# Residual of the last norm kept in the output and added there by accumulating transfers

## The chip, the cores and the metric

The kernel runs on one core of a Trainium2 chip. The metric is the device time of one execution in microseconds. Engines are called PE (TensorE), DVE (VectorE), ACT (ScalarE), POOL (GpSimd) and SP (SyncE); SP begins nearly all transfers.

## What is computed

One decoder block on x of 1024 rows by 1024 columns, float32. A token-mixing part (two kinds of attention) gives x2; then comes the channel part, at whose end the change lies:

```python
x = x + gt_a * rms_norm(y, g_attn_post[l])           # x2 below

h = rms_norm(x, g_mlp_pre[l]) * (1 + sc_m) + sh_m
y = jnp.square(jax.nn.relu(h @ w_up[l])) @ w_down[l]
x = x + gt_m * rms_norm(y, g_mlp_post[l])            # the output
```

rms_norm divides each row by the root of its mean square and multiplies by a gain. The kernel holds gt_m times the gain as one tile, `gate_m`.

## The kernel before

Rows are worked on in eight blocks of 128 (tb 0 to 7), one row to a partition. Every product is made of three float32r passes over a high and a low part of its operands (lines 2103 to 2105). The two products of the channel part are cut into quadrants and multiplied by a scheme with seven products in place of eight (P1 to P7), over eight steps h; ACT writes the high parts (L1864), DVE the low parts (L1871). Sums of the second product collect in eight tiles `yacc0` to `yacc7` of 128 x 1024, to which DVE adds each finished 128 x 512 piece from PSUM (L2161).

The order of instructions is set while the program is built. A planner (`Sched`) holds a queue for each engine, with an estimated duration, dependencies, buffers taken and given, and a priority for each step; it always emits the step that could begin first by its estimates. So a changed step can move others. On the chip each engine runs its list in order and waits on semaphores.

What the change touches:

- `out_rest(tb, ...)` ends the token-mixing part of a block. It stores x2 of the block in a scratch tensor `x2_dram[tb]` (L1724, 512 KB).
- `finish(tb, n, e)` runs when columns 512n to 512n + 511 of block tb are complete, so twice for each block. ACT squares the piece and sums each row (`f_sq`, L2178) into a column of a small tile `st3`.
- At a block's first call DVE multiplies the piece by `gate_m` in place (L2186), adds a small constant to the sum (L2182), and SP begins the load of x2 from scratch into `x2_sb` (L2191).
- At the second call DVE multiplies that piece by `gate_m` into a tile `yg` (L2198), adds the two sums (L2201), POOL raises the result to -1/2 (L2203), and DVE does for each half `x2_sb = half * power + x2_sb` in one operation (L2205). SP stores each half of 256 KB to the output (L2211).

In the last step (h = 7) the last products are P3, P7 and P4. P7 completes the first pieces of blocks 4 to 7, and P4, the very last, their second pieces, block by block.

Of the kernel before, what the change touches and what calls it, by code (L numbers as in the profile page):

```python
# [10 lines left out]
F32 = mybir.dt.float32  # L11
# [4 lines left out]
ALU = mybir.AluOpType  # L16
# [3 lines left out]
P = 128  # L20
# [3 lines left out]
TB = S // P  # L24
# [172 lines left out]
class Sched:  # L197
# [18 lines left out]
    def op(self, eng, dur, emit, deps=(), **kw):  # L216

        o = self.step(dur, emit, deps, **kw)
        o.alts = None
        if isinstance(eng, str):  # L220
            self.queue[eng].append(o)
        else:
            o.alts = dict(zip(eng, zip(dur, emit)))
            for e in eng:
                self.queue[e].append(o)
        return o.ev

    def pe_op(self, stream, dur, emit, deps=(), **kw):
        o = self.step(dur, emit, deps, **kw)
        o.alts = None  # L230
        self.pe.setdefault(stream, []).append(o)
        return o.ev
# [104 lines left out]
def t_sb(n):  # L337
    return 0.098 + 0.00083 * n


def t_as(n):
    return 0.2 + 0.00083 * n


def t_dv(n):
    return 0.066 + 0.00104 * n
# [14 lines left out]
AP_COST = 0.093  # L361
AP_DV = 0.066
# [3 lines left out]
def hybrid_block(ctx: ExitStack, tc: tile.TileContext, x, positions, w_ada, b_ada, g_attn_post, w_in, w_out,  # L366
                 g_mlp_post, w_up, w_down, ada_t, consts, out):
    nc = tc.nc
    ctx.enter_context(tc.manual_schedule())
    V, A, G, T = nc.vector, nc.scalar, nc.gpsimd, nc.tensor  # L370
    x, out = x[0], out[0]
    w_ada, w_out, w_up, w_down = w_ada[0], w_out[0], w_up[0], w_down[0]
    sc = Sched()
    op, pe_op = sc.op, sc.pe_op
# [13 lines left out]
    def ring_l(name, dtype=F32R):  # L388

        return ph2.left.tile([P, 1024], dtype, name=name, tag="left")  # L390

    def ring_r(name):

        return ph2.right.tile([P, 1024], F32, name=name, tag="right")
# [7 lines left out]
    r_stg, r_w, r_wl, r_hl = Res(NSTG), Res(WR), Res(WR + 1), Res(0)  # L402
    r_u, r_raw, r_h2 = Res(0), Res(0), Res(0)
# [12 lines left out]
    nhalf = const.tile([P, KC], F32, name="nhalf")  # L416
# [15 lines left out]
    x2_dram = [dram.tile([P, D], F32, name=f"x2_dram{i}") for i in range(TB)]  # L432
# [27 lines left out]
    def stage(name):  # L460
        if st.stgp is None:
            return ring_r(name)
        return st.stgp.tile([P, 1024], F32, name=name, tag="stg")

    def load(emit, nbytes, deps=(), takes=(), prio=5, gives=(), after=None, n=1):
        return op("SP", nbytes / 345e3, emit, deps, takes=takes, prio=prio, gives=gives, after=after, kind=n)
# [121 lines left out]
    e = op("ACT", 0.1, lambda: A.activation(cond[:], c_raw, AF.Exp, scale=-1.0), [e_c], prio=0)  # L588
# [13 lines left out]
    e = op("DVE", 1.3, f_diag, [e_cond], takes=[(r_wa, 1)], prio=0)  # L602
# [7 lines left out]
    e = pe_op("mod", 1.7, f_cps, [e, e_init], takes=[(r_t, 2)], gives=[(r_wa, 1)])  # L610
# [17 lines left out]
    cs = p0.tile([64, 3, P], F32, name="cs")  # L628
# [8 lines left out]
    e = e_pos  # L637
    for f in steps:
        e = op("DVE", 0.13, f, [e, e_c], prio=8)
# [908 lines left out]
    def out_block(tb):  # L1548
# [83 lines left out]
        def products(m):  # L1632
# [5 lines left out]
            for n, i, k in order:  # L1638
# [29 lines left out]
                else:  # L1668
# [3 lines left out]
                    ey.append(op("DVE", t_dv(512) + AP_DV, f_yb, [e, ea[n], er[1]], gives=[(r_b, 1)], prio=0))  # L1672
        me.load, me.products = load_o, products
        me.rest = lambda: out_rest(tb, b, late, ey, f_lx)
        return me

    def out_rest(tb, b, late, ey, f_lx):
        ex = load(f_lx, 524288, takes=[(r_vb if tb < 2 else r_stg, 1)], prio=-3)

        def f_sq(col, first):  # L1680
            def f():
                if first:
                    b["st"] = small.tile([P, 4], F32, name="st2", tag="st2")
                A.activation(ph2.junk[:], b["y"][:], AF.Square, accum_out=b["st"][:, col:col + 1])
            return f

        def norm(col, dep):
            bx = []

            def f1():  # L1690
                t = small.tile([P, 8], F32, name="rs_t", tag="rs_t")
                bx.append(t)
                V.tensor_scalar(t[:, :1], b["st"][:, col:col + 1], 1.0 / D, EPS, ALU.mult, ALU.add)
            def f2():
                G.tensor_tensor(b["st"][:, col + 1:col + 2], bx[0][:, :1], nhalf[:, :1], ALU.pow)

            def whole():
                f1()
                f2()
                V.tensor_copy(bx[0][:, 1:2], b["st"][:, col + 1:col + 2])  # L1700

            def joined():
                f1()
                f2()
                f_gate()
                f_res()
            if tb == TB - 1:
                if col:
                    return op("DVE", 1.0, whole, [dep], prio=-1)
                return op("DVE", 0.8 + 2 * t_dv(D), joined, [dep, ph2.e_gate, ex], gives=[(r_u, 1), (r_stg, 1)], prio=-1)  # L1710
            e = op("DVE", 0.08, f1, [dep], prio=0)
            return op("POOL", 1.4, f2, [e], prio=0)
        e = op("ACT", t_sb(D) + AP_COST, f_sq(0, True), ey, prio=1)
# [5 lines left out]
        e = norm(0, e)  # L1719
        if tb < TB - 1:  # L1720
            e = op("DVE", t_dv(D), f_gate, [e, ph2.e_gate], prio=1)
            e = op("DVE", t_dv(D), f_res, [e, ex], gives=[(r_stg, 1)] if tb > 1 else [], prio=1)
            ph2.e_res.append(e)
        e_x2[tb] = load(lambda: nc.sync.dma_start(x2_dram[tb][:], b["y"][:]), 524288, [e], prio=-2)  # L1724
        e = op("ACT", t_sb(D) + AP_COST, f_sq(2, False), [e], prio=1)
        e = norm(2, e)

# [6 lines left out]
        for kg in range(2):  # L1734
            def f_t(kg=kg):
                b["px", kg] = pt.tile([P, 4, P], F32, name="px2", tag="t")
                for k in range(4):
# [3 lines left out]
                            gives=[(r_u if tb == TB - 1 else ph2.r_xn, 1)] if kg else []))  # L1741
        half, tq = divmod(tb, TB // 2)
        for kg in range(2):
# [3 lines left out]
            def f_ev(eng, kg=kg, q=q):  # L1747
                def f():
# [12 lines left out]
            e = op(("DVE", "ACT"), (1.0, 1.2), (f_ev(V), f_ev(A)), [et[kg]] + [e_mod[g] for g in (2, 3, 4, 5)] +  # L1761
                   (e_h2[q][-1:] if tq else []),
                   takes=[(r_h2, 2)] if tq == 0 else [], gives=[(r_t, 1)], prio=1)
# [3 lines left out]
    e_x2 = {}  # L1767
# [27 lines left out]
    ml = Tok()  # L1795
# [372 lines left out]
    def finish(tb, n, e):  # L2168


        first = tb not in ml.st
        s = ml.st.setdefault(tb, Tok())
        cs = slice(512 * n, 512 * n + 512)

        def f_sq():
            if first:
                s.t = small.tile([P, 4], F32, name="st3", tag="st3", bufs=TB)
            A.activation(ph2.junk[:, :512], ml.y[tb][:, cs], AF.Square, accum_out=s.t[:, n:n + 1])  # L2178
        late = 0 if tb >= TB // 2 and not first else 100
        esq = op("ACT", t_as(512) + 0.19, f_sq, [e] + ([] if first else [s.e0]), prio=1 + late)  # L2180
        if first:
            s.e0 = op("DVE", 0.16, lambda: V.tensor_scalar(s.t[:, n:n + 1], s.t[:, n:n + 1], D * EPS, None, ALU.add),  # L2182
                      [esq], prio=3 + late)
            s.n0 = n
            s.yg = {n: lambda: ml.y[tb][:, cs]}
            s.eg = [op("DVE", t_dv(512), lambda: V.tensor_tensor(ml.y[tb][:, cs], ml.y[tb][:, cs], ml.gate[:, cs],  # L2186
                                                                 ALU.mult), [esq, ml.e_gate], prio=4 + late)]

            def f_lx():
                s.x = stage("x2_sb") if tb < TB // 2 else ring_r("x2_sb")  # L2190
                nc.sync.dma_start(s.x[:], x2_dram[tb][:])  # L2191
            r = r_stg if tb < TB // 2 else r_raw
            s.ex = load(f_lx, 524288, [e_x2[tb]], takes=[(r, 1)], prio=900 + tb)
            return

        def f_g():
            s.g = ring_l("yg", F32)
            V.tensor_tensor(s.g[:, 0:512], ml.y[tb][:, cs], ml.gate[:, cs], ALU.mult)  # L2198
        s.yg[n] = lambda: s.g[:, 0:512]
        s.eg.append(op("DVE", t_dv(512), f_g, [e, ml.e_gate], takes=[(r_u, 1)], prio=1 + late))  # L2200
        e = op("DVE", 0.16, lambda: V.tensor_tensor(s.t[:, 2:3], s.t[:, 0:1], s.t[:, 1:2], ALU.add), [esq, s.e0],  # L2201
               prio=late)
        e = op("POOL", 0.55 if tb == TB - 1 else 1.5, lambda: G.tensor_tensor(s.t[:, 3:4], s.t[:, 2:3], nhalf[:, :1], ALU.pow), [e], prio=0)  # L2203
        for i, hf in enumerate((s.n0, 1 - s.n0)):
            e1 = op("DVE", t_dv(512) + AP_DV, lambda hf=hf: V.scalar_tensor_tensor(  # L2205
                s.x[:, 512 * hf:512 * hf + 512], s.yg[hf](), s.t[:, 3:4], s.x[:, 512 * hf:512 * hf + 512],
                ALU.mult, ALU.add), [e, s.ex] + s.eg, prio=late)

            def sent(i=i):
                ml.done += i  # L2210
            load(lambda hf=hf: nc.sync.dma_start(out[tb * P:(tb + 1) * P, 512 * hf:512 * hf + 512],  # L2211
                                                 s.x[:, 512 * hf:512 * hf + 512]), 262144, [e1],
                 gives=[(r_u, 1)] if i else [], prio=-1, after=sent)

    RAW = ("11", "21", "12", "22")

# [68 lines left out]
```

## Time and profile before

| What | Value |
| --- | --- |
| Median of 3 runs | 1118.76 us (1116.28 to 1120.53) |
| The profiled execution | 1117.71 us |
| Its span, first to last instruction | 1115.9 us |
| Mean granted PE clock | 0.997 |
| Last matmul begins | 1106.41 us into the span |
| Last store begins | 1112.8 us into the span |

A row of the timeline gives the start in us from the span's beginning, the duration, the engine, the line and the operation as output <- inputs. A bracket at its end gives how long the engine sat idle before it, and what ended that. A row on a line or an operation gives min, median and max duration in ns, and the first and last start. A row on DMA issues gives the count, the size of one, and the median us from issue to landing. Durations of neighbours on one engine overlap a little, since one operation begins while the last one's writes end.

### The profile page before, as it was taken

What the parts mean: (1) busy time and instruction counts of PE and PEld (TensorE: products, weight loads), DVE (VectorE), ACT (ScalarE), POOL (GpSimd) and SP (SyncE); (2) the same over time, 40 slices, a digit from 0 to 9 for tenths busy, and PEclk for the clock granted to TensorE, in tenths of its full rate; (3) what the DMA queues carried; (4) which work ended last, traced back from release to release, by engine and by line L of the source; (5) the groups of instructions that cost most, each with busy time, mean ns of one, the idle gap of its engine ahead of it and who ended that gap; (6) DMA issues with size and microseconds to landing.
All of it is one profiled execution on the core that took longest, in us unless ns stands there. A gap on an engine that the chain in (4) does not pass through costs nothing.

```text
span 1115.9 us, 15870 instructions
## 1 busy us (share of the span) xinstructions
PE 1095.1 (98%) x5512; PEld 919.8 (82%) x5512; DVE 846.2 (76%) x1487; ACT 645.2 (58%) x1149; POOL 168.6 (15%) x215
## 2 busy tenths in 40 slices
PE   7999999999999999999999999999999999999996
PEld 6889888888998878888888888888888888888885
DVE  8975876899878976789698653898644996527998
ACT  7826576688867757587674334743145632347542
POOL 1003245456542322110000000000000000000002
PEclk9999999999999999999999999999999999999999
DMA  9767748677636517635851378511578013584104
GB/s 358 258 213 233 185 140 257 194 220 231 179 110 205 147 58 240 212 143 226 323 214 38 113 254 320 189 57 43 197 266 314 21 57 113 189 321 150 38 19 151
DMA packets 98585, 200.75 MB, mean 180 GB/s; under 512 B 8456, under 2 KB 31560, under 8 KB 98504
## 3 DMA queue, kind: packets, MB, share of 16 engines
q1 hardware_dynamic: 98504, 199.73, 53.0%
q8 instruction: 44, 0.72, 0.3%
q14 instruction: 37, 0.30, 0.1%
HBM read 157.56 MB, written 42.14 MB: 179 GB/s over the span
## 4 chain that ended last, share of the span: by engine, by line
PE 79%; DVE 10%; ACT 4%; DMA 3%; issue 3%; SPq 0%; POOL 0%; DVEq 0%; POOLq 0%; ACTq 0%
PE mlp_ps L2104 17%; PE mlp_ps L2105 17%; PE mlp_ps L2103 17%; PE pj L931 2%; PE pj L934 2%; PE pj L932 2%; PE s_ps L1215 2%; PE y_ps L1648 2%; PE y_ps L1649 2%; PE y_ps L1650 2%; PE s_ps L1269 1%; PE o_ps L1349 1%; PE o_ps L1360 1%; PE acc L931 1%; PE acc L932 1%
## 5 line engine op out<-in xcount | busy, mean ns | idle before, releaser
L2103 PE MATMUL mlp_ps<-hw 128*128 128x512 f32 x896 | 349.6, 390 | 0.0
L2104 PE MATMUL mlp_ps<-hw 128*128 128x512 f32 x896 | 348.7, 389 | 0.6 <-DVE hw L1868 0.6
L2105 PE MATMUL mlp_ps<-hw 128*128 128x512 f32 x896 | 348.6, 389 | 0.0
L2104 PEld LDWEIGHTS mlp_ps<-hw 128*128 128x128 f32 x896 | 168.2, 188 | 36.1 <-DVE hw L1868 1.0
L2103 PEld LDWEIGHTS mlp_ps<-hw 128*128 128x128 f32 x896 | 168.2, 188 | 35.4 <-issue 0.5
L2105 PEld LDWEIGHTS mlp_ps<-hw 128*128 128x128 f32 x896 | 168.2, 188 | 34.8
L1871 DVE TENSOR_TENSOR hw<-w,hw 128x1024 fp32r<-128x1024 f32 x94 | 111.7, 1221 | 106.7 <-ACT hw L1864 106.6
L1864 ACT CAST hw<-w 128x1024 fp32r<-128x1024 f32 x94 | 95.1, 1048 | 137.0 <-PE mlp_ps L2105 103.1
L2203 POOL TENSOR_TENSOR st<-st,nhalf 128x1 f32<-128x1 f32 x8 | 7.6, 957 | 601.3 <-DVE st L2201 601.3
L1337 DVE TENSOR_TENSOR ph<-pt_ps,ph 128x512 fp32r<-128x512 f32 (+1 forms) x110 | 68.9, 644 | 24.4 <-ACT ph L1333 23.8
L1864 ACT CAST hw<-u 128x1024 fp32r<-128x1024 f32 x48 | 48.7, 1051 | 64.6 <-PE mlp_ps L2105 64.6
L1333 ACT CAST ph<-pt_ps 128x512 fp32r<-128x512 f32 (+1 forms) x110 | 58.5, 555 | 25.4 <-PE pt_ps L1322 20.5
L1107 POOL TENSOR_TENSOR ada_acc<-ada_acc,wa_st 128x512 f32<-128x512 f32 x42 | 56.4, 1342 | 105.3 <-DMA qk_dram<-hl 70.9
L1871 DVE TENSOR_TENSOR hw<-u,hw 128x1024 fp32r<-128x1024 f32 x48 | 57.1, 1221 | 16.7 <-ACT hw L1864 16.7
L1245 POOL TENSOR_SCALAR p_sb<-p_sb,den 128x128 f32<-128x128 f32 (+3 forms) x64 | 51.4, 806 | 110.4 <-DVE den L1243 100.3
L931 PE MATMUL pj<-hw,w_hl 128*128 128x512 f32 x160 | 68.1, 425 | 0.0
L2161 DVE TENSOR_TENSOR yacc<-yacc,mlp_ps 128x512 f32<-128x512 f32 x96 | 62.2, 684 | 3.3 <-PE mlp_ps L2105 3.3
L934 PE MATMUL pj<-hw,w_hl 128*128 128x512 f32 x160 | 63.1, 394 | 0.0
L932 PE MATMUL pj<-hw,w_hl 128*128 128x512 f32 x160 | 63.0, 394 | 0.0
L1240 ACT ACTIVATE p_sb<-p_sb,mn 128x128 f32<-128x128 f32 (+3 forms) x64 | 49.8, 778 | 20.4 <-DVE mn L1233 18.0
L1215 PE MATMUL s_ps<-kt,qt 128*128 128x512 f32 (+2 forms) x192 | 49.6, 355 | 0.6 <-DVE mn L1233 0.4
L1648 PE MATMUL y_ps<-hw,oh 128*128 128x512 f32 x120 | 48.6, 405 | 0.1
(213 smaller groups left out, 2099.3 us busy)
## 6 DMA issues: line engine op xcount, KB each, us to landing
hw<-s_dram SPq DMA_DIRECT2D x84, 512.0 KB, 4.4
wa_st<-in_w_ada SPq DMA_DIRECT2D x32, 512.0 KB, 4.2
w<-in_w_up SPq DMA_DIRECT2D x32, 512.0 KB, 4.7
w<-in_w_down SPq DMA_DIRECT2D x32, 512.0 KB, 9.4
s_dram<-hw SPq DMA_DIRECT2D x28, 512.0 KB, 4.1
qk_dram<-hl SPq DMA_DIRECT2D x52, 256.0 KB, 4.7
kt<-qk_dram SPq DMA_DIRECT2D x40, 256.0 KB, 6.2
w_st<-in_w_in SPq DMA_DIRECT2D x18, 512.0 KB, 5.0
```

Source lines behind the costliest of these rows:

```text
L931: T.matmul(ps, wt[:, 0, c0:c0 + P], hw[:, k, 0, t], start=(k == 0), stop=False)
L932: T.matmul(ps, wt[:, 1, c0:c0 + P], hw[:, k, 0, t], start=False, stop=False)
L934: T.matmul(ps, wt[:, 0, c0:c0 + P], hw[:, k, 1, t], start=False, stop=(k == KC - 1))
L1215: T.matmul(s[:, :cw], q_t[u, h, qb // 4][:, qb % 4 * P:qb % 4 * P + P], k_t[u, h, m][:, hl, :cw], start=(hl == 0), stop=(hl == 1))
L1337: V.tensor_tensor(b["ph"][:, 1, :w], b["pt"][:, :w], b["ph"][:, 0, :w].bitcast(F32), ALU.subtract)
L1648: T.matmul(ps[:], oh, wh, start=(k == 4 * i), stop=False)
L1864: A.copy(out[j][0], flat(src[j]))
L1871: V.tensor_tensor(out[j][1], flat(src[j]), out[j][0].bitcast(F32), ALU.subtract)
L2103: T.matmul(ps[m][:], sh, mh, start=starts and k == 0, stop=False, **kw)
L2104: T.matmul(ps[m][:], sh, ml_, start=False, stop=False, **kw)
L2105: T.matmul(ps[m][:], sl, mh, start=False, stop=k == 3, **kw)
L2161: e = op("DVE", t_dv(512), lambda: V.tensor_tensor(y(), y(), ps[m][:], ALU.add), [e, ml.e_y[tb, n]], gives=gives, prio=1)
```

## The change

x2 of blocks 0 to 6 is stored in the output itself; only block 7 still goes through scratch and back. For blocks 0 to 6 both pieces of `yacc` are multiplied by `gate_m` in place; the second time this now waits for the square of the same piece, which reads it. Then ACT multiplies both halves by the row's power in place, and POOL begins one transfer of 512 KB that adds the tile to the output. These transfers are begun by POOL as the program's first. Block 7 (`own`) is computed as before, with other priorities. The planner counts 1.2 us for one begun transfer on POOL.

```diff
-        e_x2[tb] = load(lambda: nc.sync.dma_start(x2_dram[tb][:], b["y"][:]), 524288, [e], prio=-2)
+        home = x2_dram[tb][:] if tb == TB - 1 else out[tb * P:(tb + 1) * P, :]
+        e_x2[tb] = load(lambda: nc.sync.dma_start(home, b["y"][:]), 524288, [e], prio=-2)
...
-        esq = op("ACT", t_as(512) + 0.19, f_sq, [e] + ([] if first else [s.e0]), prio=1 + late)
+        own = tb == TB - 1
+        esq = op("ACT", t_as(512) + 0.19, f_sq, [e] + ([] if first else [s.e0]), prio=(-1 if own else 1) + late)
+        if own and not first:
+            def f_g():
+                s.g = ring_l("yg", F32)
+                V.tensor_tensor(s.g[:, 0:512], ml.y[tb][:, cs], ml.gate[:, cs], ALU.mult)
+            s.yg[n] = lambda: s.g[:, 0:512]
+            s.eg.append(op("DVE", t_dv(512), f_g, [e, ml.e_gate], takes=[(r_u, 1)], prio=1))
+        else:
+            if first:
+                s.yg, s.eg = {}, []
+            s.yg[n] = lambda: ml.y[tb][:, cs]
+            s.eg.append(op("DVE", t_dv(512), lambda: V.tensor_tensor(ml.y[tb][:, cs], ml.y[tb][:, cs], ml.gate[:, cs],
+                                                                     ALU.mult), [esq, ml.e_gate], prio=4 + late))
...
-            def f_lx():
-                s.x = stage("x2_sb") if tb < TB // 2 else ring_r("x2_sb")
-                nc.sync.dma_start(s.x[:], x2_dram[tb][:])
-            r = r_stg if tb < TB // 2 else r_raw
-            s.ex = load(f_lx, 524288, [e_x2[tb]], takes=[(r, 1)], prio=900 + tb)
+            if own:
+                def f_lx():
+                    s.x = ring_r("x2_sb")
+                    nc.sync.dma_start(s.x[:], x2_dram[tb][:])
+                s.ex = load(f_lx, 524288, [e_x2[tb]], takes=[(r_raw, 1)], prio=900 + tb)
             return
...
+        e = op("POOL", 0.55 if own else 1.5, lambda: G.tensor_tensor(s.t[:, 3:4], s.t[:, 2:3], nhalf[:, :1], ALU.pow),
+               [e], prio=0)
+        ends = []
         for i, hf in enumerate((s.n0, 1 - s.n0)):
...
+            if own:
+                ends = [op("DVE", t_dv(512) + AP_DV, lambda hf=hf, hs=hs: V.scalar_tensor_tensor(
+                    s.x[:, hs], s.yg[hf](), s.t[:, 3:4], s.x[:, hs], ALU.mult, ALU.add), [e, s.ex] + s.eg, prio=0)]
+                load(lambda hs=hs: nc.sync.dma_start(out[tb * P:(tb + 1) * P, hs], s.x[:, hs]), 262144, ends,
+                     gives=[(r_u, 1)] if i else [], prio=-1, after=sent)
+            else:
+                ends.append(op("ACT", t_as(512) + AP_COST, lambda hf=hf: A.mul(s.yg[hf](), s.yg[hf](), s.t[:, 3:4]),
+                               [e] + s.eg, prio=2 + late))
+        if not own:
+            op("POOL", 1.2, lambda: G.dma_start(out[tb * P:(tb + 1) * P, :], ml.y[tb][:], accum_op=ALU.add), ends,
+               prio=5, after=sent)
```

Lines 2178 and 2201 of before are 2179 and 2206 of the changed file; its gate products stand on L2193 (in place) and L2186 (block 7's second), the power on L2208, the scaling on ACT on L2222, the accumulating transfers on L2225, and block 7's last operation and stores on L2217 and L2219. PE's list is the same row for row, and the other lists differ only in what follows.

POOL at the program's end, before (`st3_9792` to `st3_9826` are blocks 0 to 3, `st3_10088` to `st3_10110` blocks 4 to 7):

```order
L2203 TENSOR_TENSOR st3_9826<-st3_9826,nhalf_68 128x1
L2203 TENSOR_TENSOR st3_10088<-st3_10088,nhalf_68 128x1
L2203 TENSOR_TENSOR st3_10097<-st3_10097,nhalf_68 128x1
L2203 TENSOR_TENSOR st3_10103<-st3_10103,nhalf_68 128x1
L2203 TENSOR_TENSOR st3_10110<-st3_10110,nhalf_68 128x1
```

POOL at the program's end, after (`st3_9818` is block 3, `st3_10070` to `st3_10092` blocks 4 to 7):

```order
L2208 TENSOR_TENSOR st3_9818<-st3_9818,nhalf_68 128x1
L2225 DMA out_x<-yacc0_6762 128x1024
L2225 DMA out_x<-yacc1_6768 128x1024
L2225 DMA out_x<-yacc2_6773 128x1024
L2225 DMA out_x<-yacc3_6782 128x1024
L2208 TENSOR_TENSOR st3_10070<-st3_10070,nhalf_68 128x1
L2208 TENSOR_TENSOR st3_10077<-st3_10077,nhalf_68 128x1
L2225 DMA out_x<-yacc4_6984 128x1024
L2208 TENSOR_TENSOR st3_10085<-st3_10085,nhalf_68 128x1
L2225 DMA out_x<-yacc5_6993 128x1024
L2208 TENSOR_TENSOR st3_10092<-st3_10092,nhalf_68 128x1
L2225 DMA out_x<-yacc6_6998 128x1024
```

The powers, which stood alone, now stand between transfers: block 7's behind block 5's transfer, with block 6's transfer behind it.

ACT's last rows before, the squares of blocks 4 to 7 (first pieces, then second pieces):

```order
L2178 ACTIVATE junk2_4891,st3_10110<-yacc7_7003 128x512
L2178 ACTIVATE junk2_4891,st3_10088<-yacc4_6984 128x512
L2178 ACTIVATE junk2_4891,st3_10097<-yacc5_6993 128x512
L2178 ACTIVATE junk2_4891,st3_10103<-yacc6_6998 128x512
L2178 ACTIVATE junk2_4891,st3_10110<-yacc7_7003 128x512
```

ACT's last rows after:

```order
L2179 ACTIVATE junk2_4891,st3_10070<-yacc4_6984 128x512
L2179 ACTIVATE junk2_4891,st3_10077<-yacc5_6993 128x512
L2222 ACTIVATE yacc4_6984<-yacc4_6984,st3_10070 128x512 x2
L2179 ACTIVATE junk2_4891,st3_10085<-yacc6_6998 128x512
L2222 ACTIVATE yacc5_6993<-yacc5_6993,st3_10077 128x512 x2
L2179 ACTIVATE junk2_4891,st3_10092<-yacc7_7003 128x512
L2222 ACTIVATE yacc6_6998<-yacc6_6998,st3_10085 128x512 x2
```

The scaling of a block stands behind the square of the next block, which waits for PE and for DVE's addition.

More of the change, by code (lines that the diff above doesn't have):

```diff
@@ L2184, in finish @@
             s.n0 = n
-            s.yg = {n: lambda: ml.y[tb][:, cs]}
-            s.eg = [op("DVE", t_dv(512), lambda: V.tensor_tensor(ml.y[tb][:, cs], ml.y[tb][:, cs], ml.gate[:, cs],
-                                                                 ALU.mult), [esq, ml.e_gate], prio=4 + late)]
-            def f_lx():
-                s.x = stage("x2_sb") if tb < TB // 2 else ring_r("x2_sb")
-                nc.sync.dma_start(s.x[:], x2_dram[tb][:])
-            r = r_stg if tb < TB // 2 else r_raw
@@ L2193, in finish @@
-            s.ex = load(f_lx, 524288, [e_x2[tb]], takes=[(r, 1)], prio=900 + tb)
-            return
[L2196 to L2200, printed above, removed]
+            if own:
[3 more added lines that the diff above has]
+                s.ex = load(f_lx, 524288, [e_x2[tb]], takes=[(r_raw, 1)], prio=900 + tb)
@@ L2201, in finish @@
+            return
         e = op("DVE", 0.16, lambda: V.tensor_tensor(s.t[:, 2:3], s.t[:, 0:1], s.t[:, 1:2], ALU.add), [esq, s.e0],
-               prio=late)
-        e = op("POOL", 0.55 if tb == TB - 1 else 1.5, lambda: G.tensor_tensor(s.t[:, 3:4], s.t[:, 2:3], nhalf[:, :1], ALU.pow), [e], prio=0)
+               prio=-1 if own else late)
+        e = op("POOL", 0.55 if own else 1.5, lambda: G.tensor_tensor(s.t[:, 3:4], s.t[:, 2:3], nhalf[:, :1], ALU.pow),
+               [e], prio=0)
+        ends = []
@@ L2204, in finish @@
         for i, hf in enumerate((s.n0, 1 - s.n0)):
-            e1 = op("DVE", t_dv(512) + AP_DV, lambda hf=hf: V.scalar_tensor_tensor(
-                s.x[:, 512 * hf:512 * hf + 512], s.yg[hf](), s.t[:, 3:4], s.x[:, 512 * hf:512 * hf + 512],
-                ALU.mult, ALU.add), [e, s.ex] + s.eg, prio=late)
+            hs = slice(512 * hf, 512 * hf + 512)
             def sent(i=i):
                 ml.done += i
-            load(lambda hf=hf: nc.sync.dma_start(out[tb * P:(tb + 1) * P, 512 * hf:512 * hf + 512],
-                                                 s.x[:, 512 * hf:512 * hf + 512]), 262144, [e1],
-                 gives=[(r_u, 1)] if i else [], prio=-1, after=sent)
+            if own:
[6 more added lines that the diff above has]
+                               [e] + s.eg, prio=2 + late))
```

## Prediction

> **What bounds the kernel now.** I read the head of the page first (busy shares), then the chain that ended last.
>
> ```profile
> span 1115.9 us, 15870 instructions
> PE 1095.1 (98%) x5512; PEld 919.8 (82%) x5512; DVE 846.2 (76%) x1487; ACT 645.2 (58%) x1149; POOL 168.6 (15%) x215
> PE 79%; DVE 10%; ACT 4%; DMA 3%; issue 3%; SPq 0%; POOL 0%; DVEq 0%; POOLq 0%; ACTq 0%
> ```
>
> PE is busy for nearly the whole span, so DVE and DMA work beside PE costs nothing. Whether that holds where the diff works shows in the busy time of the last stretches (columns: PE, PEld, DVE, ACT, POOL, granted clock, DMA share, GB/s).
>
> ```profile
> 1084.00:1098.00 14.00, 14.00 (x63) 11.62 (x62) 13.56 (x24) 7.25 (x18) 4.25 (x4) 1.00 0.25 94
> 1098.00:1109.00 11.00, 8.80 (x39) 6.95 (x37) 10.96 (x25) 2.61 (x8) 2.79 (x3) 1.00 0.46 168
> 1109.00:1116.00 7.00, 0.00 (x0) 0.00 (x0) 3.09 (x6) 0.37 (x2) 0.55 (x1) 0.70 0.40 150
> ```
>
> Until 1098 PE has no gap. From 1098 DVE is full (10.96 of 11) while PE runs dry, and the last 7 us have no PE at all. So only the tail behind the last matmul can move. Its timeline, cut to the rows that matter (start, duration, engine, line):
>
> ```profile
> 1100.97 0.39 PE L2105 MATMUL mlp_ps<-hw 128*128 128x512 f32 x1
> 1101.48 0.68 DVE L2161 TENSOR_TENSOR yacc<-yacc,mlp_ps 128x512 f32<-128x512 f32 x1
> 1102.26 0.63 ACT L2178 ACTIVATE junk<-yacc 128x512 bf16<-128x512 f32 x1 [2.00 <-DVE yacc L2161]
> 1103.69 0.39 PE L2105 MATMUL mlp_ps<-hw 128*128 128x512 f32 x1
> 1104.68 0.68 DVE L2161 TENSOR_TENSOR yacc<-yacc,mlp_ps 128x512 f32<-128x512 f32 x1
> 1106.41 0.39 PE L2105 MATMUL mlp_ps<-hw 128*128 128x512 f32 x1
> 1107.88 0.68 DVE L2161 TENSOR_TENSOR yacc<-yacc,mlp_ps 128x512 f32<-128x512 f32 x1
> 1108.65 0.63 ACT L2178 ACTIVATE junk<-yacc 128x512 bf16<-128x512 f32 x1 [2.47 <-DVE yacc L2161]
> 1109.19 0.18 ACT L2178 ACTIVATION_READ_ACCUMULATOR junk<-yacc 128x1 f32 x1
> 1109.20 0.74 DVE L2205 SCALAR_TENSOR_TENSOR x_sb<-yacc,st,x_sb 128x512 f32<-128x512 f32 x1
> 1109.86 0.74 DVE L2205 SCALAR_TENSOR_TENSOR x_sb<-yg,st,x_sb 128x512 f32<-128x512 f32 x1
> 1110.53 0.15 DVE L2201 TENSOR_TENSOR st<-st 128x1 f32<-128x1 f32 x1
> 1110.76 0.55 POOL L2203 TENSOR_TENSOR st<-st,nhalf 128x1 f32<-128x1 f32 x1 [2.39 <-DVE st L2201]
> 1112.01 0.75 DVE L2205 SCALAR_TENSOR_TENSOR x_sb<-yg,st,x_sb 128x512 f32<-128x512 f32 x1
> ```
>
> The blocks of rows 5, 6 and 7 leave PE at 1101.36, 1104.08 and 1106.80 (start plus 0.39). Block 5's add starts 0.12 later. Block 6's starts 0.60 late and block 7's 1.08 late, because DVE still works on older blocks. Block 7's sum of squares is read by 1109.37, but the add of its two parts (L2201) waits for block 6's two L2205 until 1110.53. DVE's backlog is thus what stands between PE's end and the last store, about 2 us.
>
> **The change, part by part.** Durations of the operations that go or come:
>
> ```profile
> L2205 DVE SCALAR_TENSOR_TENSOR x_sb<-yacc,st,x_sb x8: 743/746/752, 1089.1 to 1111.3; 128x512 f32<-128x512 f32 x8
> L1100 ACT ACTIVATE wa_st<-wa_st,cond x42: 707/720/747, 90.1 to 314.6; 128x512 f32<-128x512 f32 x42
> L2203 POOL TENSOR_TENSOR st<-st,nhalf x8: 543/930/1602, 1086.4 to 1110.8; 128x1 f32<-128x1 f32 x8
> L1107 POOL TENSOR_TENSOR ada_acc<-ada_acc,wa_st x42: 1272/1292/2332, 90.9 to 316.1; 128x512 f32<-128x512 f32 x42
> L2191 SPq DMA_DIRECT2D x_sb<-x_dram x8: 319/320/595, 1002.0 to 1060.7; - x8
> L2211 SPq DMA_DIRECT2D out_x<-x_sb x16: 332/332/338, 1089.9 to 1112.8; - x16
> out_x<-x_sb SPq DMA_DIRECT2D x16, 256.0 KB, 2.0
> x_dram<-y_sb SPq DMA_DIRECT2D x8, 512.0 KB, 3.0
> x_sb<-x_dram SPq DMA_DIRECT2D x8, 512.0 KB, 10.4
> ```
>
> *Stores of x2 to the output.* Same seven 512 KB stores at the same places of SP's queue: nothing. *Seven x2 loads gone* (issued 1002 to 1061, PE full): nothing, and what SP has behind them (w loads, then stores) keeps PE full either way. *DVE* loses 14 L2205 x 0.746 = 10.4 us; all but block 6's pair run while PE does, and count only through the backlog above. *ACT* gains 14 scalings; L1100 is the same operation and shape, 0.72, so 10 us on an engine that is 24% busy from 1098 on (2.61 of 11). *POOL* gains seven DMA issues, *SP* loses fourteen stores of 256 KB.
>
> By the order of rows shown with the change, POOL has block 7's power behind block 5's transfer and block 6's transfer as its last work. On ACT each pair of scalings stands behind the next block's square, and the transfer waits for the pair.
>
> *Block 7's chain.* Without L2205 of older blocks DVE adds block 7 at 1106.92 (PE's end plus the 0.12 of block 5), until 1107.60. The square and its readout take 0.1 + 0.72 (1107.88 + 0.68 to 1109.37 now is 0.81), to 1108.42; L2206 to 1108.60; the power at 1108.65 with the 0.55 of an idle DVE, to 1109.20; two L2217 (1.42 between 1111.34 and 1112.76) to 1110.67. Its last store is issued near 1110.7 instead of 1112.8 and lands 2.0 later: 1112.7 instead of 1114.8. By itself that is -2.1 us.
>
> *The accumulating transfers.* No row shows a DMA from POOL, or one that adds. Two unknowns. First the issue on POOL, g: at least SP's 0.33, at most about the 1.29 of POOL's dearest common row; I take 1.0, nearest to the 0.93 that a small POOL instruction costs in this tail. Second the data time t of 512 KB on all engines. Queue rows of the trace (packets, MB, share of 16 engines), first of 1085 to 1116 (stores alone, 8 x 512 KB), then of 1000 to 1062 (loads, 13 x 512 KB):
>
> ```profile
> q1 hardware_dynamic: 2304, 4.20, 36.6%
> q1 hardware_dynamic: 2135, 6.79, 30.7%
> ```
>
> Share times window over count: a store takes 0.366 x 31 / 8 = 1.42 us and a load 0.307 x 62 / 13 = 1.46. Adding in the output means reading it and writing it: t is 1.42 if the read hides behind the write, 2.9 if they follow each other, and more if each packet waits for its read. I take 2.9. A plain 512 KB store lands 3.0 after issue, so 1.6 is fixed. Landing = issue + (g - 0.33) + t per transfer in the queue + 1.6.
>
> When each is issued follows from the rows above and three more:
>
> ```profile
> 1086.87 2.35 DVE L1871 TENSOR_TENSOR hw<-u,hw 128x1024 fp32r<-128x1024 f32 x2
> 1092.02 2.12 POOL L2203 TENSOR_TENSOR st<-st,nhalf 128x1 f32<-128x1 f32 x2 [3.52 <-DVE st L2201]
> 1101.04 0.93 POOL L2203 TENSOR_TENSOR st<-st,nhalf 128x1 f32<-128x1 f32 x1 [6.91 <-DVE st L2201]
> ```
>
> Blocks 0 to 3 from about 1091.5 (two powers, 2.12 us, after L1871's end at 1089.2 and the two sums behind it); block 4 at 1104.4 (its pair starts at 1102.99, when block 5's square is read, and takes 2 x 0.72); block 5 at 1107.1 (square of block 6 ends at 1105.67); block 6 at 1109.8 (pair from 1108.42). With g = 1 and t = 2.9: block 6 alone lands at 1115.0, blocks 4 to 6 one behind another at 1104.4 + 0.67 + 8.7 + 1.6 = 1115.4, all seven at 1091.5 + 0.67 + 20.3 + 1.6 = 1114.1. The latest, 1115.4, takes over from block 7's store and is 0.6 later than 1114.8 now. **Sum: +0.6 us**: the 2.1 us that DVE gives are spent on transfers that begin late and do double work. Block 7's power is not delayed: POOL is free at 1107.1 + g, before 1108.65 as long as g is under 1.5.
>
> By the Trainium skill ("DMA: Bandwidth & Descriptors", Anatomy of one DMA, SWDGE path) a DMA from GpSimd costs about 2.0 us plus bytes / 436 GB/s, by which block 6 would land at 1113.0 and the sum would be -1.8; it prices no accumulation, and no run so far shows one.
>
> **The rivals.**
>
> *R1, reads hidden* (t = 1.42): block 6 lands at 1109.8 + 0.67 + 1.42 + 1.6 = 1113.5, sum -1.3; with g = 0.33, block 7's 1112.7 and 1112.8 decide, -2.0. For it: loads and stores overlap elsewhere in the trace. Against: here a write needs its own read.
>
> *R2, the adding is slow, and it ends slower.* Seven transfers in a queue end at 1093.8 + 7t. That passes today's 1114.8 at t = 3.0 and is 0.5% later at t = 3.8. A read that is partly waited for suffices: eight 4 KB rows per engine and a fixed 1.6 us per round trip would give up to 13 us each, +70 in all, if nothing overlapped; t = 4.5 gives 1125.3, +10.5. Loads landing 10.4 us after issue under load show that waits of that size occur.
>
> *R3, POOL held by DVE.* The power costs 0.55 with DVE idle and 0.93 beside it (min and median above). If descriptor writing is held the same way until DVE pauses, block 5's issue waits for the add and the gate of block 7 (to 1108.2) and block 6's for L2217 (to 1110.7): block 7's power slips 0.5, block 6 lands 0.9 later, sum +1.1 to +1.5. The Trainium skill ("SBUF — State Buffer", SBUF: two separate sides) has such a lock, but for DVE operations in a 2-port mode or against GpSimd operations that read SBUF; by it R3 would hold only if the additions of this tail ran in such a mode, and no row here shows one.
>
> *R4, no effect*: a one-time cost of POOL's first DMA would hide, since POOL has nothing due between 1095.5 (four issues from 1091.5) and block 4's power, at 1101.0 now.
>
> **How the numbers follow.** Forecast 0.50 (own range -0.5 to +3 us), R1 0.16, R2 0.24 (past t = 3.8), R3 with R4 0.10. The sums are made against the profiled execution, 1117.71; the median of the runs shown is 1118.76, so the time is 1118.8 + 0.6 = 1119.4. Low: R1's -2.0 and 1.3 of the runs' own spread (1116.28 to 1120.53): 1115.5. High: R2 with t = 4.0, 1093.8 + 28 = 1121.8, +7.0, rounded up to 1127 for the same spread; the slower half of R2 lies above. No mechanism here gains 5.6 us (0.5%, about what a measurement of this kernel tells from no change): the whole tail behind PE is 9 us. Faster 0.02, same 0.74, slower 0.24.
>
> **What would show it.** Right: block 7's L2217 end near 1110.7, L2225 issues at about 1 us each, and the chain ends in a DMA to the output that began on POOL, landing about 5 us after issue. Wrong: seven transfers still draining long after 1115 (R2), or SP's store ending last (R1). PE's end moving from 1106.8 would upset everything above.

## The result and the profile after

The changed kernel takes 1120.93 us (median of 22 executions) against 1117.34 us for the kernel before: ratio 1.0029, 95% interval 1.0022 to 1.0036, that is 3.2 us more (2.5 to 4.0). One of the 22 executions took 3883 us and is left out of the ratio. The forecast was +0.6 us and "the same within 0.5%"; the size is wrong, the second holds.

The execution profiled took 1122.16 us, its span is 1120.3 us. PE ends in it at 1108.50 us (1108.11 + 0.39), 1.7 us later than in the profile before. In the executions profiled below PE's end lies anywhere from 1105.60 to 1108.50 us, and the kernel that only moves x2's home ended PE at 1107.56 us with the time of before. All these kernels have the same list for PE. So everything below is told as the **tail**: from the end of the last matmul to the end of the span. It was 9.1 us before (1106.80 to 1115.9) and is 11.8 us after (the expectations below read it as 11.9).

Busy time of the engines in the last stretches (columns as in the prediction):

```profile
1098.00:1108.50 10.50, 10.49 (x47) 8.36 (x45) 7.28 (x17) 5.94 (x14) 3.66 (x4) 1.00 0.94 165
1108.50:1120.30 11.80, 0.00 (x0) 0.00 (x0) 2.95 (x5) 1.99 (x5) 2.36 (x4) 0.64 0.81 167
```

DVE, which had 10.96 us of 11 before, now has 7.28 of 10.5. In its place the DMA engines are full: a share of 0.94 while PE still runs, and 0.81 over a tail in which DVE works for 2.95 us. Their chain is seen in the timeline of the tail:

```profile
1103.88 0.63 ACT L2179 ACTIVATE junk<-yacc 128x512 bf16<-128x512 f32 x1 [2.00 <-DVE yacc L2162]
1104.51 1.33 ACT L2222 ACTIVATE yacc<-yacc,st 128x512 f32<-128x512 f32 x2
1106.13 0.89 POOL L2225 DMA_DIRECT2D out_x<-yacc  x1 [0.33 <-ACT yacc L2222]
1108.53 0.69 DVE L2162 TENSOR_TENSOR yacc<-yacc,mlp_ps 128x512 f32<-128x512 f32 x1 [0.42 <-PE mlp_ps L2106]
1108.84 0.88 POOL L2225 DMA_DIRECT2D out_x<-yacc  x1 [0.31 <-ACT yacc L2222]
1110.07 0.16 DVE L2206 TENSOR_TENSOR st<-st 128x1 f32<-128x1 f32 x1
1110.32 0.56 POOL L2208 TENSOR_TENSOR st<-st,nhalf 128x1 f32<-128x1 f32 x1 [0.59 <-DVE st L2206]
1111.56 0.88 POOL L2225 DMA_DIRECT2D out_x<-yacc  x1 [0.68 <-ACT yacc L2222]
1111.58 0.75 DVE L2217 SCALAR_TENSOR_TENSOR x_sb<-yg,st,x_sb 128x512 f32<-128x512 f32 x1
1111.69 1.00 SPq L2219 DMA_DIRECT2D out_x<-x_sb  x2
```

DVE takes block 7 at once now (0.03 us after PE's end as modelled), and its last operation ends 3.8 us after PE's end (1111.58 + 0.75 less 1108.50) instead of 6.0. That is the 2.1 us that were forecast. But block 6's transfer begins at the same moment, and it takes long. The transfers that POOL begins, and the DMA queues from 1085 us on:

```profile
L2225 POOL DMA_DIRECT2D out_x<-yacc x7: 881/1046/1545, 1093.2 to 1111.6; - x7
DMA to landing us min/median/max: 5.3/7.4/12.8
q0 software_dynamic: 1008, 3.67, 53.1%
q1 hardware_dynamic: 288, 0.52, 3.7%
out_x<-x_sb SPq DMA_DIRECT2D x2, 256.0 KB, 4.1
```

The first and second row belong to the line L2225; the queue rows (queue, packets, MB, share of the 16 engines) are shares of a window of 40 us. The seven adding transfers hold the 16 engines for 0.531 x 40 / 7 = 3.03 us each. The last three land 5.3, 5.8 and 7.4 us after their issue; block 6's lands at 1111.56 + 7.4 = 1119.0, 1.3 us before the span's end. Block 7's stores are of 256 KB each; the one whose landing is on record lands 4.1 us after issue, where such stores took 2.0.

The share of time in which the DMA engines were busy, in tenths, in 40 slices of 0.4 us from 1104 us on:

```profile
DMA  9999542129895989999999999989899997420000
```

Blocks 0 to 3 drain until about 1107; from 1107.6 to about 1118 the engines have hardly a pause. That is some 10.4 us, and three adding transfers with block 7's stores make 3 x 3.03 + 1.42 = 10.5.

### The profile page after: what moved, and what is told of

Same layout as the page of the kernel before. It is cut to its first block, busy times and chain, and to the rows that moved or that the text cites. A ratio compares the mean times of both kernels' runs of the same rounds, so it can differ in the third digit from the quotient of the medians.

```text
span 1120.3 us, 15838 instructions
## 1 busy us (share of the span) xinstructions
PE 1095.4 (98%) x5512; PEld 919.9 (82%) x5512; DVE 837.9 (75%) x1473; ACT 653.6 (58%) x1163; POOL 173.5 (15%) x222
## 4 chain that ended last, share of the span: by engine, by line
PE 81%; DVE 9%; ACT 3%; DMA 3%; issue 2%; SPq 1%; POOL 0%; POOLq 0%; ACTq 0%; DVEq 0%
PE mlp_ps L2106 17%; PE mlp_ps L2105 17%; PE mlp_ps L2104 17%; PE pj L931 2%; PE pj L934 2%; PE pj L932 2%; PE s_ps L1215 2%; PE y_ps L1648 2%; PE y_ps L1649 2%; PE y_ps L1650 2%; PE o_ps L1349 1%; PE s_ps L1269 1%; PE acc L931 1%; PE o_ps L1360 1%; PE acc L932 1%
## 5 line engine op out<-in xcount | busy, mean ns | idle before, releaser
L2208 POOL TENSOR_TENSOR st<-st,nhalf 128x1 f32<-128x1 f32 x8 | 7.0, 874 | 593.7 <-DVE st L2206 593.6
L2162 DVE TENSOR_TENSOR yacc<-yacc,mlp_ps 128x512 f32<-128x512 f32 x96 | 62.5, 683 | 7.8 <-PE mlp_ps L2106 7.8
```

Source lines behind the costliest of these rows:

```text
L2162: e = op("DVE", t_dv(512), lambda: V.tensor_tensor(y(), y(), ps[m][:], ALU.add), [e, ml.e_y[tb, n]], gives=gives, prio=1)
```

## The experiments

Two theories. **A (data):** an adding transfer holds all DMA engines about twice as long as a plain one, and from block 4's issue on the engines work almost without a pause, so their queue ends the program. **B (issue):** a transfer begun by POOL is late by itself, through its software descriptors and a slow completion. And of the kernel before, whether DVE's backlog was what its tail consisted of, or only its own chain (**C**).

| Kernel | Tail, us | Ratio to before (95%) |
| --- | --- | --- |
| before | 9.1 | 1 |
| changed | 11.8 | 1.0029 (1.0022 to 1.0036) |
| plain transfers from POOL | 8.2 | 0.9992 (0.9980 to 1.0004) |
| plain transfers from SP | 7.8 | 0.9996 (0.9986 to 1.0006) |
| changed, block 7's stores thinned | 10.1 | 1.0009 (0.9998 to 1.0019) |
| adding for blocks 0 to 5 | 11.2 | 1.0010 (0.9999 to 1.0021) |
| adding for blocks 0 to 4 | 8.2 | 0.9995 (0.9985 to 1.0005) |
| adding for blocks 0 to 3 | 7.8 | 0.9987 (0.9975 to 0.9999) |
| the same, DVE's end reordered | 7.7 | 0.9990 (0.9981 to 0.9999) |
| x2's home moved alone | 9.1 | 1.0002 (0.9993 to 1.0010) |

**Without the addition.**

```diff
-            op("POOL", 1.2, lambda: G.dma_start(out[...], ml.y[tb][:], accum_op=ALU.add), ends,
+            op("POOL", 1.2, lambda: G.dma_start(out[...], ml.y[tb][:]), ends,
```

> The seven transfers that POOL begins only store the scaled tile; the addition of x2 is left out for blocks 0 to 6. All lists keep their order. The tail, from the end of the last matmul to the span's end, is 9.1 us before and 11.9 changed. Theory A (data): an adding 512 KB transfer holds the 16 DMA engines for 3.0 us, a plain one for 1.4, and from block 4's issue on the engines are never idle; so here each block's transfer is done before the next, block 6's and block 7's data (2.8 us) run from 3.7 us after PE's end, tail about 9.0, some 2.9 us faster than the changed kernel and level with before. Rival B (issue): a transfer begun on POOL is late by itself, with its descriptors written in software and a slow completion, 7.5 us from issue to landing; then the tail stays at 11.5 to 11.9 and the time at +3 us over before.

Rows of its L2225 and of its queues from 1085 us on, as those above:

```profile
L2225 POOL DMA_DIRECT2D out_x<-yacc x7: 533/570/772, 1091.0 to 1109.3; - x7
DMA to landing us min/median/max: 2.9/3.6/4.9
q0 software_dynamic: 1008, 3.67, 23.4%
out_x<-x_sb SPq DMA_DIRECT2D x2, 256.0 KB, 2.2
```

The same bytes in the same packets hold the engines 0.234 x 40 / 7 = 1.34 us each instead of 3.03, and block 6's transfer lands after 3.6 us instead of 7.4. The tail falls by 3.6 us, to 8.2; expected were 9.0. The last three issues are where they were, 2.4 us before and 0.3 and 3.1 us after PE's end. The cost is in the addition, not in POOL's beginning the transfer: B falls.

**SP begins them.**

```diff
-            op("POOL", 1.2, lambda: G.dma_start(out[...], ml.y[tb][:], accum_op=ALU.add), ends,
-               prio=5, after=sent)
+            load(lambda: nc.sync.dma_start(out[...], ml.y[tb][:]), 524288, ends, prio=-1, after=sent)
```

> As the run with plain transfers from POOL (blocks 0 to 6 stored without the addition of x2), but SP begins the seven 512 KB transfers. It separates who begins a transfer from what it does. If a transfer from POOL costs only its longer issue (0.57 against 0.34 us), the tail is 0.2 to 0.3 us shorter than the 8.2 us of the run from POOL and the time the same within the measurement (about -1 us to before). Rival: descriptors made in software also slow the data; then the tail falls by 1 us or more.

```profile
L2225 SPq DMA_DIRECT2D out_x<-yacc x7: 332/333/356, 1090.5 to 1110.3; - x7
DMA to landing us min/median/max: 2.7/2.7/2.7
```

The trace has one landing here, the first transfer's: 2.7 us after issue, against 2.9 from POOL (the minimum above). The tail is 0.4 us shorter, and the two times can't be told apart. Who begins a plain transfer hardly matters here.

**Block 7's stores thinned.**

```diff
-                load(lambda hs=hs: nc.sync.dma_start(out[tb * P:(tb + 1) * P, hs], s.x[:, hs]), 262144, ends,
+                load(lambda hs=hs: nc.sync.dma_start(out[tb * P:(tb + 1) * P, hs.start:hs.start + 16], s.x[:, hs.start:hs.start + 16]), 8192, ends,
```

> Block 7's two stores of 256 KB are cut to 16 columns each (the rest of block 7 is left out of the output). Theory A: they share the engines with the adding transfers and cost 1.4 us there, so the tail falls from 11.9 to about 10.5 us and the time to about +1.5 us over before. Rival B: block 6's transfer lands 7.5 us after issue whatever runs beside it; tail 11.9, time +3 us.

Block 6's issue and landing here, in two rows:

```profile
1111.38 0.88 POOL L2225 DMA_DIRECT2D out_x<-yacc  x1 [0.67 <-ACT yacc L2222]
DMA to landing us min/median/max: 5.6/5.6/5.6
```

Block 6's transfer lands 1.8 us sooner after its issue (5.6 for 7.4) and the tail is 1.7 us shorter, with nothing taken away but two plain stores. Expected by A were 1.4. The time says the same: +1.0 us over before (-0.2 to +2.1) in place of +3.2. The stores share the engines with block 6's transfer.

**Fewer adding blocks.** For n = 4, 5 and 6 blocks from n on are finished as before; only the last block keeps its special priorities.

```diff
-        home = x2_dram[tb][:] if tb == TB - 1 else out[tb * P:(tb + 1) * P, :]
+        home = x2_dram[tb][:] if tb >= n else out[tb * P:(tb + 1) * P, :]
...
-        own = tb == TB - 1
+        own, end = tb >= n, tb == TB - 1
```

n = 6:

> Blocks 6 and 7 are finished as before (DVE and plain stores), blocks 0 to 5 by adding transfers. Theory A: from block 4's issue (2.4 us before PE's end, data 0.6 later) the engines have 2 x 3.0 + 2 x 1.4 = 8.9 us of work, landing 1.4 and end 1.1 later: tail 9.6, time about +0.5 us over before. Rival B: block 5 is issued 0.3 us after PE's end and lands 7.5 us later: tail 8.9; the two stores of block 7 from SP end a tail of 7.5.

n = 5:

> Blocks 5 to 7 finished as before, blocks 0 to 4 by adding transfers. Theory A: block 4's adding transfer holds the engines from 1.8 us before PE's end to 1.2 after it; blocks 5 to 7 are stored later than that, so nothing queues. DVE's list ends with block 7's addition, product and sum ahead of block 6's last pair, so its last store is issued near 4.2 us after PE's end: tail 7.3 to 7.5, time about 1.7 us under before. Rival B (any late adding transfer ends the program): block 4's lands about 5.4 us after its issue, that is 3 us after PE's end, and can't end it either; so both say faster, and B is told apart only if the tail is over 8.5.

n = 4:

> Blocks 4 to 7 are finished as before, only blocks 0 to 3 by adding transfers. Theory A: the four adding transfers are done 2 us before PE's end and cost nothing, DVE has no backlog of older blocks when PE ends, and block 7's last store is issued about 4.3 us after PE's end instead of 6.0: tail about 7.5 us, time 1.6 us under before (ratio 0.9986). Rival C: the last chain of before was not DVE's backlog but its own length, so the tail stays at 9.1 and the time at before's.

With n = 6 the tail is 11.2 us where A expected 9.6, though the time (+1.1 us, -0.1 to +2.3) allows the +0.5. Its DMA rate, 40 slices of 0.4 us from 1102 us on, shows what A lacks:

```profile
GB/s 236 184 72 41 31 31 143 51 123 143 174 164 195 236 205 102 205 143 256 205 164 230 374 394 394 399 389 374 138 26 26 26 26 0 0 0 0 0 0 0
```

The engines together are done at 1113.6, 8.0 us after PE's end at 1105.60; by A's terms it would be 7.1. Block 4's data begin only near 1104.4, 1.2 us after its issue at 1103.2, where A has 0.6. Then for 1.6 us a rest drains at 26 GB/s, about a sixteenth of the rate of all (374 to 399), and its packets follow each other one at a time: one engine is late with its share of rows. Why it was late in this execution was not tried.

With n = 5 the tail is 8.2 where 7.3 to 7.5 was expected, and the time 0.6 us under before (-1.7 to +0.6) where 1.7 was. The last store is issued 4.4 us after PE's end (4.2 expected) and lands after 2.8 us instead of 2.0, behind block 4's data and five stores: the engines move 375 to 408 GB/s from 1111 to 1114 us. With n = 4 the adding transfers are over before the tail:

```profile
1107.12 0.39 PE L2106 MATMUL mlp_ps<-hw 128*128 128x512 f32 x1
1107.77 0.68 DVE L2162 TENSOR_TENSOR yacc<-yacc,mlp_ps 128x512 f32<-128x512 f32 x1
1109.70 0.15 DVE L2206 TENSOR_TENSOR st<-st 128x1 f32<-128x1 f32 x1
1109.77 0.68 DVE L2186 TENSOR_TENSOR yg<-yacc,gate_m 128x512 f32<-128x512 f32 x1
1109.92 0.93 POOL L2208 TENSOR_TENSOR st<-st,nhalf 128x1 f32<-128x1 f32 x1 [2.33 <-DVE st L2206]
1111.56 0.75 DVE L2217 SCALAR_TENSOR_TENSOR x_sb<-yg,st,x_sb 128x512 f32<-128x512 f32 x1
out_x<-yacc POOLq DMA_DIRECT2D x4, 512.0 KB, 10.6
out_x<-x_sb SPq DMA_DIRECT2D x8, 256.0 KB, 2.0
```

Block 7's sum stands 2.2 us after PE's end (1109.70 less 1107.51; 3.7 before), the last operation ends after 4.8 us (6.0 before), and the stores whose landing is on record take the 2.0 us of before, though the four adding transfers ahead of them take 10.6. The tail is 7.8 (7.5 expected), the time 1.5 us under before (0.1 to 2.8). So the tail of before was not fixed by the length of block 7's own chain, and C falls.

Two things made that chain end sooner. Block 7's add begins 0.26 us after PE's end instead of 1.08, because DVE has less older work: this is the backlog, 0.8 us. And block 7's product with `gate_m` stands behind its sum (L2186 at 1109.77), where before it stood ahead of block 6's last pair and so of the sum:

```profile
1108.59 0.69 DVE L2198 TENSOR_TENSOR yg<-yacc,gate_m 128x512 f32<-128x512 f32 x1
```

This lets the sum come 0.7 us sooner, and POOL's power, which now runs beside that product, takes 0.93 instead of 0.55. What is left of it, some 0.3 us, is a matter of order. No run gave the kernel before that order, or block 7's priorities, without adding transfers, so how much of the 1.5 us could be had without them is open. This version has the lowest ratio of those run, by an interval that barely leaves 1 out.

**DVE's end reordered** (n = 4): block 6's last two operations also depend on block 7's sum.

```diff
+                    ... [e, s.ex] + s.eg + ([st7] if tb == TB - 2 else []), prio=0 if end else late)]
```

> As the run with blocks 4 to 7 finished as before, and the last operations of block 6 on DVE wait for block 7's sum, so that block 7's product and sum stand ahead of them. If DVE's order behind PE's end is what is left, the last store is issued near 4.2 us after PE's end instead of 4.9, tail 7.2 instead of 7.8, ratio to before about 0.998. Rival: the chain through POOL's power decides anyway; tail 7.8.

```profile
1109.09 1.00 POOL L2211 TENSOR_TENSOR st<-st,nhalf 128x1 f32<-128x1 f32 x1 [1.95 <-DVE st L2207]
1110.92 0.74 DVE L2220 SCALAR_TENSOR_TENSOR x_sb<-yg,st,x_sb 128x512 f32<-128x512 f32 x1
```

The last operation ends 4.6 us after PE's end (1107.05), 0.4 later than expected: block 5's pair still held DVE when block 7's piece came, and POOL's power beside DVE takes 1.00. The ratio, 0.9990, is that of the run without it within the intervals, and the 0.998 that was expected lies just outside (0.9981 to 0.9999). A gain of 0.1 us in the tail is not one that these runs can show.

**One part alone:** x2 goes through the output and back, all else as before.

```diff
-... nc.sync.dma_start(x2_dram[tb][:], b["y"][:]) ...
+... nc.sync.dma_start(x2_dram[tb][:] if tb == TB - 1 else out[tb * P:(tb + 1) * P, :], b["y"][:]) ...
...
-                nc.sync.dma_start(s.x[:], x2_dram[tb][:])
+                nc.sync.dma_start(s.x[:], x2_dram[tb][:] if tb == TB - 1 else out[tb * P:(tb + 1) * P, :])
```

> One part alone: x2 of blocks 0 to 6 is stored in the output and loaded back from there; all else as before. All theories: no cost, ratio 1.000 within 0.001, tail 9.1.

As expected: tail 9.1, ratio 1.0002 (0.9993 to 1.0010).

## Why the prediction was right, and where it was off

- **Only the tail can move, and PE's end stays put:** right. The order of PE is untouched, and moving x2's home alone costs nothing. The prediction named a moved end of PE as what would upset it, and in the changed kernel's profile PE ends 1.7 us later. But for every kernel of the table the change of the tail lies inside the interval of the change of time, so no shift of PE's end by the change itself can be seen.
- **Block 7's chain, -2.1 us:** right. Its last operation ends 3.8 us after PE's end instead of 6.0.
- **Issue times:** right. Blocks 4, 5 and 6 are issued 2.4 us before and 0.3 and 3.1 us after PE's end; forecast were 2.4 before and 0.3 and 3.0 after.
- **g = 1.0 and t = 2.9:** right, with 0.88 (of the last three) and 3.03. An adding transfer takes what reads and writes would take that follow each other; that they do so is not shown, only the sum of the two. R1 did not come, and neither did the slow R2 with t past 3.8. For a plain 512 KB transfer from POOL an estimate by the Trainium skill (DMA: Bandwidth & Descriptors, Anatomy of one DMA, SWDGE path) is 3.2 us, from about 2.0 us plus bytes / 436 GB/s. Measured were 2.9 at least and 3.6 in the median, which is near it; an adding one is not, with 5.3 at least.
- **R3, POOL held by DVE:** did not come. Block 5's and block 6's issues took 0.88 each beside DVE's L2162 and L2217. Of the plain transfers all but the first took 0.53 to 0.58 to issue, with DVE idle or beside these lines. The Trainium skill (SBUF — State Buffer, SBUF: two separate sides) ties its lock to DVE operations in a 2-port mode, or with two inputs in SBUF against a GpSimd operation that reads SBUF. These rows do not go against it, but they do not test it either, since no row shows such a mode.
- **The queue's end, 0.6 us later than before: the step that failed.** Block 6's transfer lands 10.5 us after PE's end (1119.0 less 1108.50) where the sum had 8.6 (1115.4 less 1106.80). The sum queued the adding transfers behind each other, and left block 7's own two stores out of that queue, although it had them issued within a microsecond of block 6's transfer. They are 512 KB, 1.42 us of the engines by the prediction's own row, and 1.7 us of the tail by the run that thins them. That accounts for most of the 2.1 us by which the tail (+2.7 for +0.6) was missed. The 0.4 us left is about what three transfers of 3.03 us take more than three of 2.9; no run tests that part by itself. So block 6's transfer landed 7.4 us after its issue and not the "about 5" that the prediction named as its sign, though blocks 4 and 5 did, with 5.3 and 5.8.
- **The chances:** the time lies in "the same" and in the range; of the forecast's own range (-0.5 to +3 us) it is just outside. That "same" came true says little of the mechanism: a tail of 9 us in 1118 leaves room for little else, and the range reached from 1115.5 to 1127. The direction, slower, came out of the queue that was summed, and there the sum was short.

## What to carry to other kernels

A transfer that adds in memory spares an engine one operation but here it occupies the DMA engines more than twice as long as a plain store (3.03 against 1.34 us for 512 KB), so it is for data that is ready while the DMA engines are idle and something else still has to finish, not for the last blocks. When the end of a program is a queue, list everything that is issued into it, also transfers that the change leaves as they were. And try the change on the early part of the work alone: here the version with blocks 0 to 3 came out 1.5 us under before, and the whole change 3.2 us over.

## What the runs showed of the hardware that was not expected

- POOL needs longer to begin an adding transfer than a plain one of the same shape: 0.88 against 0.53 us at least. POOL's first adding transfers, four in a row, together took 3.74.
- A single DMA engine can be late with its share: 1.6 us at 26 GB/s at the end of the run with n = 6. The span went on until 1116.8, 1.6 us after that engine was done.
- PE's end differs by up to 2.9 us between executions of kernels whose PE lists are equal (1105.60 to 1108.50), about the size of the whole effect; only the tail of each profile, and many executions, made it readable.
